# State space mixer: outputs in two kinds of PSUM bank, state tiles made once, second half's transposes in two kinds

## The chip, the core and the metric

The kernel runs on one core of one Trainium2 chip. The metric is device time in microseconds (us) of one launch, the median of several. The core has a matrix engine (TensorE, here PE), three other compute engines (VectorE or DVE, ScalarE or ACT, GpSimd or POOL), and SyncE (SP), whose queue issues the DMAs. PE writes its results to PSUM, eight banks of 128 partitions x 512 float32; DVE and ACT read them out.

## The reference

A transformer block with two mixers, a state space one (S5) and sparse attention, and two feed-forward parts. The change lies in S5. It has 32 groups of 16 channels with 64 complex states each, over 512 time steps:

```python
bu_re = jnp.einsum('bsgc,gpc->bsgp', ug, bbar_re)      # ug: input, 32 groups of 16 channels
bu_im = jnp.einsum('bsgc,gpc->bsgp', ug, bbar_im)
_, _, xr, xi = lax.associative_scan(combine, (a_seq_re, a_seq_im, bu_re, bu_im), axis=1)
y = (jnp.einsum('bsgp,gcp->bsgc', xr, c_re) - jnp.einsum('bsgp,gcp->bsgc', xi, c_im) + d_skip * ug)
yg = jax.nn.gelu(y)
out = yg * jax.nn.sigmoid(yg @ w_glu + b_glu)
```

Beside it stand the gates that later mix the two mixers' outputs: a sigmoid of the normed input times 2048 columns of `w_in`.

## The kernel before

**Gates.** They are computed in 16 units of 128 columns, `gt0_0` to `gt0_7` and `gt1_0` to `gt1_7`. A unit is 24 matmuls of 128x512 that all add into one PSUM bank: eight slices of the inner dimension, each with high part times high part (L211), low times high (L212) and high times low (L213). Weights come by DMA (`raw`); ACT rounds them to the high part `wh`, DVE takes the rest as `wl`. When the 24 are done, DVE scales the bank into `gt` (one 128x512 operation, L192 `gt<-ps_mm,rbs`), which frees the bank, and ACT applies the sigmoid.

**State space.** `s5_half` (L638) handles 16 of the 32 groups at a time, in two tiles `jt` of 8. It is called with `hf` 0 and 1, and the code has it stand between the gates: gates 0 and 1, half 0, gates 2 to 7, half 1, gates 8 to 15, then `glu`. In a half:
- `products` forms the input matrix `T1` (s5A, s5B) and the output matrix `CA` (s5CAr, s5CAi), with a PSUM bank for one factor.
- T1 is transposed on PE (L688) and copied to `W1` by ACT; the products L698 and L699 and the transposes L702 make the kernel `KT` for the four time steps within a chunk. POOL adds the skip term to KT (L734, L735), and ten small DMAs on SP's queue spread it to `G` (L741).
- DVE forms the powers `s5P`.
- For each jt: matmuls L749 of W1 with the input give two banks `wr` and `wi`; DVE turns them by the powers (`turn`, four 128x512 operations), adds and subtracts (two more), runs 8 scans of 128x128 (L773) back into the banks, turns them again (four), and writes the states to `X` (s5Xr, s5Xi, two). Column 0 of X is zero, and POOL sets it (L777).
- The output `py` is 96 small matmuls in one bank (L787): G with the input, CAr with s5Xr, CAi with s5Xi, for four time steps. ACT takes the gelu (`yg`, L790).

**Banks.** The eight banks are dealt by kind (L413): four "mm", one "sm", three "aux". A tile takes the next bank of its kind in the order in which the code asks, and its first writer waits until the bank's former tile has been read for the last time. Gate units are "mm". In a half all of T1, bc, the transposes and KT's products are "aux", wr and wi are "aux" for an even jt and "mm" for an odd one, and py of either jt is "sm".

**What sets the order.** A scheduler orders each engine's instructions from the code, the data they need and the banks; the code adds a few orderings without waits (the `turn` and `before` names). Within one kind of bank, tiles keep the order of the code. An engine works its instructions in order: one that waits holds all behind it.

Of the kernel before, what the change touches and what calls it, by code (L numbers as in the profile page):

```python
# [179 lines left out]
class Kern:  # L180
# [459 lines left out]
    def s5_half(self, hp, hf, A, Gp, m4, u4, s5d, ura):  # L640
        nc, I = self.nc, self.I
# [4 lines left out]
        def tile(shape, name, bufs=1):  # L646
            return hp.tile(shape, F32, name=name, tag=name, bufs=bufs)
# [35 lines left out]
        W1 = [tile([128, 8, 128], n) for n in ("s5W1r", "s5W1i")]  # L683
        for c in range(2):
            for q in range(2):
                tp = self.mmtile((128, 512), "aux")
                for i in range(4):
                    ins = nc.tensor.transpose(tp[:, 128 * i:128 * i + 128], T1[c][:, 4 * q + i], self.ident)  # L688
                    self.tc.add_manual_dep(ins.ins, self.before, NOSYNC, reason="order")
                self.act(W1[c][:, 4 * q:4 * q + 4], tp)  # L690
# [20 lines left out]
        n = 1  # L711
        while n < 128:

            m = min(n, 127 - n)
            if m > 0:
                by = lambda c: PP[:, c:c + 1, :, n:n + 1].to_broadcast([128, 2, 8, m])
                x, o = PP[:, :, :, 1:m + 1], PP[:, :, :, n + 1:n + m + 1]
# [20 lines left out]
        for d in range(4):  # L738
            j = 3 - d
            for s1 in range(4 - d):  # L740
                nc.sync.dma_start(G[32 * s1:32 * s1 + 32, :, s1 + d, :], KT[32 * j:32 * j + 32])  # L741

        for jt in (2 * hf, 2 * hf + 1):
            ur = ura[:, jt]
            q4 = slice(4 * (jt % 2), 4 * (jt % 2) + 4)
            wr, wi = (self.mmtile((128, 512), ("aux", "mm")[jt % 2]) for _ in range(2))
            for c, w in ((0, wr), (1, wi)):
                for pl in range(4):
                    nc.tensor.matmul(w[:, 128 * pl:128 * pl + 128], W1[c][:, q4.start + pl], ur[:, pl],  # L749
                                     start=True, stop=True)  # L750
            Pr, Pi = P[0][:, q4].rearrange("p a b -> p (a b)"), P[1][:, q4].rearrange("p a b -> p (a b)")

            t2 = lambda n: tile([128, 2, 512], n)
            ac = t2("s5A") if jt % 2 == 0 else t2("s5W1r")
            zc = t2("s5C") if jt % 2 == 0 else t2("s5W1i")
            ta, tc = ac[:, 0], ac[:, 1]
            zr, zi = zc[:, 0], zc[:, 1]

            def turn():

                self.tt(ta, wr, Pr, mul)
                self.tt(wr, wr, Pi, mul)
                self.tt(tc, wi, Pr, mul)
                self.tt(wi, wi, Pi, mul)

            turn()
            self.tt(zr, ta, wi, add)
            self.tt(zi, tc, wr, sub)
            for z, s in ((zr, wr), (zi, wi)):
                for pl in range(4):  # L770
                    pr = 4 * jt + pl
                    sl = slice(128 * pl, 128 * pl + 128)
                    nc.vector.tensor_tensor_scan(s[:, sl], m4[:, pr:pr + 1].to_broadcast([128, 128]), z[:, sl], 0.0,  # L773
                                                 mul, add)
            X = [tile([128, 4, 129], n, 1) for n in ("s5Xr", "s5Xi")]
            for x in X:
                nc.gpsimd.memset(x[:, :, 0:1], 0.0)  # L777
            v = lambda a: a.rearrange("p (a b) -> p a b", a=4)
            turn()
            self.tt(X[0][:, :, 1:], v(ta), v(wi), sub)  # L780
            self.tt(X[1][:, :, 1:], v(tc), v(wr), add)

            py = self.mmtile((128, 512), "sm")
            for st in range(4):
                for i, (w, x) in enumerate(((G, ur), (CA[0], X[0]), (CA[1], X[1]))):
                    for pl in range(4):
                        nc.tensor.matmul(py[32 * pl:32 * pl + 32, 128 * st:128 * st + 128], w[:, q4.start + pl, st],  # L787
                                         x[:, pl, 0:128], start=i == 0, stop=i == 2, tile_position=(0, 32 * pl))
            yg = self.gp.tile([128, T], F32, name="yg", tag="yg", bufs=2)
            self.act(yg.rearrange("p (c s) -> p s c", s=4), py.rearrange("p (s c) -> p s c", s=4), AF.Gelu_apprx_tanh)  # L790
            self.split_to(self.y_ssm[0][:, jt], self.y_ssm[1][:, jt], yg)
# [251 lines left out]
    def nsa_cmp(self, p):  # L1043
# [3 lines left out]

        X = p.tile([128, 4, 8, 32], F32, name="cX")
        for half in range(2):
            ps = self.mmtile((128, 512), "aux")  # L1050
            for i2 in range(2):
                i = 2 * half + i2
                for j in range(4):
                    nc.tensor.matmul(ps[:, 256 * i2 + 64 * j:256 * i2 + 64 * j + 64],
                                     qk[j][:, 128 * i:128 * i + 128], self.kcbd, start=True, stop=True)
            self.tt(X[:, 2 * half:2 * half + 2], ps.rearrange("p (a h c) -> p a h c", a=2, h=8),
                    self.biasc[:, 2 * half:2 * half + 2], OP.add)
# [1064 lines left out]
```

## Time and profile before

| | us |
|---|---|
| three runs | 1603.66, 1607.11, 1603.70 |
| median | 1603.7 |
| profiled execution | 1606.45 |
| its span on the engines | 1604.7 |
| PE busy in the span | 1551.7 (97%) |
| DVE busy | 1107.8 (69%) |
| half 0, half 1 and gates 2 to 15, up to the start of `glu` | 54 to 161.28 |

The profiled execution's time is 1.75 above its span and 2.75 above the median of the runs. PE is busy over most of the length; the state space mixer and its gates lie between about 46 and 170 us of the span, and the other 1430 us hold the rest of the block. A matmul's row shows some 0.4 us though the next starts 0.23 later: PE works them in a pipeline, so their cost is read from start to start.

### The profile page before, as it was taken

To read this page: it belongs to the slowest core of one execution; us is meant where nothing else is said; L and a number is where in the kernel's file an instruction comes from. 1 tells how busy PE (TensorE), PEld (TensorE's weight loads), DVE (VectorE), ACT (ScalarE), POOL (GpSimd) and SP (SyncE) were. 2 spreads that over 40 slices of the span, in tenths; PEclk is the share of its full clock that TensorE was granted. 3 is DMA by queue.
4 is the path that set the end of the run, shared out by engine and by line. 5 is a ranking of instruction groups with operands and counts; after the bars stand their busy time and mean duration, and the time that the engine had idled before them with its cause. 6 is when DMAs were issued, how large, how long until landed. Compare 5 with 4: busy or idle time off the path is not lost.

```text
span 1604.7 us, 22771 instructions
## 1 busy us (share of the span) xinstructions
PE 1551.7 (97%) x8577; PEld 1296.0 (81%) x8577; DVE 1107.8 (69%) x2055; ACT 764.3 (48%) x1405; POOL 385.0 (24%) x327
## 2 busy tenths in 40 slices
PE   7999997999999999999999999999989999999997
PEld 6778786677888888888888888878879888888886
DVE  8887546676679754863436777478877798676745
ACT  5453536563444213452346777646654664343322
POOL 1110124113000000000020001314320897556552
PEclk9999999999999999999999999999999999999998
DMA  5222411004356764833222111111211322232322
GB/s 192 82 74 67 133 56 47 14 21 133 103 199 214 245 197 130 258 111 103 82 65 71 33 51 54 47 56 64 66 59 66 102 95 92 98 100 92 96 86 82
DMA packets 58733, 157.84 MB, mean 98 GB/s; under 512 B 11904, under 2 KB 18816, under 8 KB 58496
## 3 DMA queue, kind: packets, MB, share of 16 engines
q1 hardware_dynamic: 58624, 156.40, 30.4%
q8 instruction: 67, 1.10, 0.3%
q14 instruction: 42, 0.34, 0.1%
HBM read 152.57 MB, written 2.10 MB: 96 GB/s over the span
## 4 chain that ended last, share of the span: by engine, by line
PE 81%; DVE 11%; ACT 5%; issue 2%; POOL 1%; DMA 1%; SPq 0%; DVEq 0%; ACTq 0%
PE ps_mm L211 23%; PE ps_mm L213 22%; PE ps_mm L212 22%; PE ps_sm L1129 2%; DVE wl L192 2%; DVE caccm L201 2%; PE ps_mm L1118 1%; PE ps_aux L1574 1%; ACT L189 1%; ACT wh L189 1%; PE ps_sm L787 1%; DVE caccf L201 1%; PE ps_aux L1563 1%; PE ps_aux L1096 1%; PE ps_sm L1590 0%
## 5 line engine op out<-in xcount | busy, mean ns | idle before, releaser
L189 ACT ACTIVATE wh<-raw 128x1024 fp32r<-128x1024 f32 (+3 forms) x234 | 236.8, 1013 | 498.7 <-PE ps_mm L212 361.6
L192 DVE TENSOR_TENSOR wl<-raw,wh 128x1024 fp32r<-128x1024 f32 (+2 forms) x162 | 196.7, 1215 | 99.3 <-ACT wh L189 93.5
L201 DVE SCALAR_TENSOR_TENSOR caccf<-ps_mm,cwf,caccf 128x441 f32<-128x441 f32 (+2 forms) x278 | 188.5, 695 | 30.9 <-ACT ctapf L189 24.8
L192 POOL TENSOR_TENSOR wl<-raw,wh 128x1024 fp32r<-128x1024 f32 (+2 forms) x72 | 160.7, 2233 | 158.7 <-ACT wh L189 158.6
L213 PE MATMUL ps_mm<-h4H,wl 128*128 128x512 f32 (+1 forms) x352 | 131.2, 375 | 0.0
L212 PE MATMUL ps_mm<-h4L,wh 128*128 128x512 f32 (+1 forms) x352 | 131.1, 375 | 0.0
L211 PE MATMUL ps_mm<-h4H,wh 128*128 128x512 f32 (+1 forms) x352 | 129.7, 377 | 0.6 <-DVE caccf L201 0.4
L192 POOL TENSOR_TENSOR rr<-rv,nhalf 128x2 f32<-128x2 f32 x9 | 8.5, 946 | 431.3 <-DVE rv L198 431.3
L211 PE MATMUL ps_mm<-h2H,wh 128*128 128x512 f32 (+1 forms) x280 | 103.8, 372 | 0.0
L213 PE MATMUL ps_mm<-h2H,wl 128*128 128x512 f32 (+1 forms) x280 | 103.6, 371 | 0.0
L212 PE MATMUL ps_mm<-h2L,wh 128*128 128x512 f32 (+1 forms) x280 | 103.6, 371 | 0.0
L211 PE MATMUL ps_mm<-aH,wh 128*128 128x512 f32 (+1 forms) x272 | 102.6, 377 | 0.5 <-DVE x L192 0.5
L213 PE MATMUL ps_mm<-aH,wl 128*128 128x512 f32 (+1 forms) x272 | 102.7, 378 | 0.0
L212 PE MATMUL ps_mm<-aL,wh 128*128 128x512 f32 (+1 forms) x272 | 102.4, 377 | 0.0
L1265 DVE CUSTOM_DVE_ANT_0 msc<-wmod,cB,cols 128x1024 bf16<-128x1024 f32 x64 | 82.0, 1282 | 21.1 <-DMA wmod<-in_wmod 20.7
L211 PE MATMUL ps_mm<-hH,wh 128*128 128x512 f32 x216 | 85.2, 402 | 8.2 <-ACT hH L189 8.2
L213 PE MATMUL ps_mm<-hH,wl 128*128 128x512 f32 x216 | 85.4, 396 | 1.5 <-DVE wl L192 1.5
L212 PE MATMUL ps_mm<-hL,wh 128*128 128x512 f32 x216 | 85.4, 396 | 0.0
L213 PEld LDWEIGHTS ps_mm<-h4H,wl 128*128 128x128 f32 x352 | 66.2, 188 | 12.3
L212 PEld LDWEIGHTS ps_mm<-h4L,wh 128*128 128x128 f32 x352 | 66.2, 188 | 12.3 <-DVE h4L L201 0.4
L211 PEld LDWEIGHTS ps_mm<-h4H,wh 128*128 128x128 f32 x352 | 65.0, 188 | 13.4 <-issue 0.8
L211 PE MATMUL ps_mm<-faH,wh 128*128 128x512 f32 (+1 forms) x194 | 72.3, 373 | 0.0
(548 smaller groups left out, 4039.2 us busy)
## 6 DMA issues: line engine op xcount, KB each, us to landing
raw<-in_wup SPq DMA_DIRECT2D x76, 512.0 KB, 3.5
wmod<-in_wmod SPq DMA_DIRECT2D x48, 512.0 KB, 4.3
raw<-in_wdn SPq DMA_DIRECT2D x32, 512.0 KB, 3.5
raw<-in_win SPq DMA_DIRECT2D x28, 512.0 KB, 3.3
raw<-in_wout SPq DMA_DIRECT2D x8, 512.0 KB, 3.5
raw<-in_wdn2a SPq DMA_DIRECT2D x8, 512.0 KB, 3.5
raw<-in_wdn2b SPq DMA_DIRECT2D x8, 512.0 KB, 3.4
raw<-in_wdn2c SPq DMA_DIRECT2D x8, 384.0 KB, 3.2
```

Source lines behind the costliest of these rows:

```text
L189: return self.nc.scalar.activation(o, i, f, **k)
L192: return (e or self.nc.vector).tensor_tensor(o, a, b, op)
L201: return self.nc.vector.scalar_tensor_tensor(o, a, s, b, op0, op1)
L211: mm(ps, wh, xh, start=start, stop=False)
L212: mm(ps, wh, xl, start=False, stop=False)
L213: ins = mm(ps, wl, xh, start=False, stop=stop)
L787: nc.tensor.matmul(py[32 * pl:32 * pl + 32, 128 * st:128 * st + 128], w[:, q4.start + pl, st], x[:, pl, 0:128], start=i == 0, stop=i == 2, ...
L1096: nc.tensor.matmul(S[:, :n2], self.qs[:, 2 * j + g, c], self.ks[:, 2 * br + g, :n2], start=True, stop=False)
L1118: nc.tensor.transpose(tp[:, 128 * b:128 * b + 128], P[g, i][:, 128 * b:128 * b + 128], self.ident)
L1129: nc.tensor.matmul(O[64 * g:64 * g + 64, 128 * i:128 * i + 128], self.V[:, b, c:c + 64], PT[g][:, 128 * b:128 * b + 128], start=br == 0 an ...
L1265: ins = nc.vector.tensor_tensor_reduce(sc, w, cB[:, c], 1.0, bm[:, m:m + 1], OP.mult, OP.add, acc)
L1563: nc.tensor.matmul(ps[k0:k0 + m, j, c:c + m], e[:, k0:k0 + m], e[:, q0:q0 + m], start=True, stop=True, tile_position=(0, k0), skip_group_c ...
```

## The change

1. In the second half two of the four transposed tiles of T1 (q = 1) go to "mm" banks and not to "aux".
2. The state tiles X are made once, in the first half, and their zero column is set once. Before, every jt made them and set the column.
3. py of an odd jt goes to an "mm" bank; only the even jt's goes to "sm".

```diff
@@ s5_half: transposes of T1
         for c in range(2):
             for q in range(2):
-                tp = self.mmtile((128, 512), "aux")
+                tp = self.mmtile((128, 512), ("aux", "mm")[hf and q])
@@ s5_half: before the loop over jt
+        if hf == 0:
+
+            self.s5X = [tile([128, 4, 129], n, 1) for n in ("s5Xr", "s5Xi")]
+            for x in self.s5X:
+                nc.gpsimd.memset(x[:, :, 0:1], 0.0)
         for jt in (2 * hf, 2 * hf + 1):
...
-            X = [tile([128, 4, 129], n, 1) for n in ("s5Xr", "s5Xi")]
-            for x in X:
-                nc.gpsimd.memset(x[:, :, 0:1], 0.0)
+            X = self.s5X
...
-            py = self.mmtile((128, 512), "sm")
+            py = self.mmtile((128, 512), ("sm", "mm")[jt % 2])
```

Lines below the insertion have other numbers afterwards: L749 becomes L754, L773 becomes L778, L787 becomes L790.

The change also moves instructions. The numbers behind names tell tiles apart. First PE in the first half, before: `ps_aux_668` and `669` are wr and wi of jt 0, `ps_mm_757` and `758` those of jt 1, `ps_sm_704` is py of jt 0, `ps_mm_852` and `885` are the banks of gates 2 and 3.

```order
L211 MATMUL ps_mm_852<-hH_78,wh_848 128x512
...
L702 MATMUL ps_aux_567<-ident_76,s5ks_576 128x128 [waits Activation_49]
L212 MATMUL ps_mm_852<-hL_79,wh_848 128x512
...
L702 MATMUL ps_aux_580<-ident_76,s5ks_589 128x128 [waits Activation_49]
...
L213 MATMUL ps_mm_852<-hH_78,wl_849 128x512
L211 MATMUL ps_mm_885<-hH_78,wh_881 128x512 [waits DVE_49]
...
L749 MATMUL ps_aux_668<-ur_123,s5W1r_540 128x128 [waits DVE_49,PE_49,Activation_49]
...
L749 MATMUL ps_aux_669<-ur_123,s5W1i_541 128x128 [waits DVE_49]
...
L787 MATMUL ps_sm_704<-ur_123,s5G_656 32x128 [waits DMAHW3_49,Pool_49]
```

The same place of the changed kernel: `ps_aux_672` and `673` are wr and wi of jt 0, `ps_mm_789` is py of jt 1, `ps_mm_848`, `881` and `914` are the banks of gates 2, 3 and 4.

```order
L702 MATMUL ps_aux_567<-ident_76,s5ks_576 128x128 [waits Activation_49]
L702 MATMUL ps_aux_580<-ident_76,s5ks_589 128x128 [waits Activation_49]
L754 MATMUL ps_aux_672<-ur_123,s5W1r_540 128x128 [waits DVE_49,PE_49,Activation_49]
...
L754 MATMUL ps_aux_673<-ur_123,s5W1i_541 128x128 [waits DVE_49]
...
L790 MATMUL ps_sm_704<-ur_123,s5G_656 32x128 [waits DMAHW3_49,Pool_49]
...
L790 MATMUL ps_mm_789<-ur_123,s5G_656 32x128 x4
L211 MATMUL ps_mm_848<-hH_78,wh_844 128x512
...
L211 MATMUL ps_mm_881<-hH_78,wh_877 128x512 [waits DVE_49]
...
L211 MATMUL ps_mm_914<-hH_78,wh_910 128x512 [waits DVE_49]
```

The 44 matmuls of gates 2 and 3 that stood among and behind L702, ahead of L749, now stand behind the first matmuls of both py. In before four "mm" tiles are live here (wr, wi and two gate banks in turn); now py of jt 1 holds a third bank for as long, the gates have one bank left, and gates 3, 4 and 5 each start with a wait for DVE's read of the gate ahead. The second half has the same form: the first matmul of gate 8 follows the first four of py of jt 3, and gates 9, 10 and 11 each wait for DVE's read of the gate ahead.

DVE at the same place, before:

```order
L192 TENSOR_TENSOR ps_aux_645<-s5Ap_367,ps_aux_518 128x512 [waits Activation_49]
L192 TENSOR_TENSOR gt0_2_402<-ps_mm_852,rbs_124 128x512 [waits PE_49]
L201 SCALAR_TENSOR_TENSOR ps_aux_645<-s5t_644,ps_aux_645 128x512 [waits DVE_49]
...
L192 TENSOR_TENSOR s5A_678<-ps_aux_669,s5P_593 128x512 [waits PE_49]
L192 TENSOR_TENSOR ps_aux_669<-ps_aux_669,s5P_593 128x512
L192 TENSOR_TENSOR gt0_3_403<-ps_mm_885,rbs_124 128x512 [waits PE_49]
...
L773 SCALAR_TENSOR_TENSOR ps_mm_757<-s5s_301,s5W1i_768 128x128 [waits DVE_49]
L773 SCALAR_TENSOR_TENSOR ps_mm_758<-s5s_301,s5W1i_768 128x128
L192 TENSOR_TENSOR wl_948<-raw_945,wh_947 128x1024 [waits DMAHW5_49,Activation_49]
L192 TENSOR_TENSOR gt0_4_404<-ps_mm_918,rbs_124 128x512 [waits PE_49]
```

And of the changed kernel:

```order
L778 SCALAR_TENSOR_TENSOR ps_mm_758<-s5s_301,s5W1i_768 128x128
L192 TENSOR_TENSOR gt0_2_402<-ps_mm_848,rbs_124 128x512 [waits PE_49]
L778 SCALAR_TENSOR_TENSOR ps_aux_672<-s5s_301,s5C_683 128x128 [waits DVE_49]
...
L192 TENSOR_TENSOR wl_944<-raw_941,wh_943 128x1024 [waits DMAHW5_49,Activation_49]
...
L778 SCALAR_TENSOR_TENSOR ps_aux_673<-s5s_301,s5C_683 128x128 [waits DVE_49]
L192 TENSOR_TENSOR s5W1r_767<-ps_mm_757,s5P_593 128x512 [waits DVE_49]
...
L192 TENSOR_TENSOR ps_aux_673<-ps_aux_673,s5P_593 128x512
L192 TENSOR_TENSOR gt0_3_403<-ps_mm_881,rbs_124 128x512 [waits PE_49]
L192 TENSOR_TENSOR wl_977<-raw_974,wh_976 128x1024 [waits DMAHW6_49,Activation_49]
```

The read of gate 2 now follows the first two of the 16 scans, and that of gate 3 the other 14 scans, one `wl`, one `s5nci` (L197) and the eight operations of the second turns, where gates 2, 3 and 4 were read among the operations ahead of the third scan. In the second half gate 8 is read after four scans, and gate 9 after the other twelve, a `wl` and the second turns. `gt0_4` comes after the X tiles, 7 large and some small operations of half 1.

## Rows read from the trace of the kernel before

**Rows 1.** The page: span, busy time and share of each engine
```profile
span 1604.7 us, 22771 instructions
PE 1551.7 (97%) x8577; PEld 1296.0 (81%) x8577; DVE 1107.8 (69%) x2055; ACT 764.3 (48%) x1405; POOL 385.0 (24%) x327
```

**Rows 2.** Waits of PE, 40 to 190 us: total us, times, longest us
```profile
PE ps_sm L787 <- ACT yg L189: 1.7, 1, 1.7
PE ps_aux L688 <- ACT s5W1r L189: 1.7, 2, 1.0
PE ps_mm L213 <- DVE wl L192: 1.5, 1, 1.5
...
PE ps_aux L688 <- POOL s5Xi L777: 0.9, 1, 0.9
PE ps_sm L787 <- DVE s5Xr L192: 0.6, 1, 0.6
```

**Rows 3.** Timeline of PE, pieces of 54 to 162: start us, us, instruction
```profile
55.38 0.27 PE L702 MATMUL ps_aux<-ident,s5ks 128*128 128x128 f32 x1
...
55.95 0.39 PE L211 MATMUL ps_mm<-hH,wh 128*128 128x512 f32 x1
56.18 0.39 PE L212 MATMUL ps_mm<-hL,wh 128*128 128x512 f32 x1
...
65.40 1.05 PE L749 MATMUL ps_aux<-ur,s5W1r 128*128 128x128 f32 x8
...
103.48 0.66 PE L688 MATMUL ps_aux<-ident,s5A 128*128 128x128 f32 x4
...
108.69 0.48 PE L211 MATMUL ps_mm<-hH,wh 128*128 128x512 f32 x1
...
161.28 0.40 PE L211 MATMUL ps_mm<-ysH,wh 128*128 128x512 f32 x1
```

**Rows 4.** Timeline of DVE, pieces of 61 to 76
```profile
61.44 0.68 DVE L192 TENSOR_TENSOR ps_aux<-s5Ap,ps_aux 128x512 f32<-128x512 f32 x1
62.03 0.68 DVE L192 TENSOR_TENSOR gt<-ps_mm,rbs 128x512 f32<-128x512 f32 x1
...
74.34 0.74 DVE L773 TENSOR_TENSOR_SCAN ps_mm<-s5s,s5W1i 128x128 f32<-128x128 f32 x2
74.99 1.21 DVE L192 TENSOR_TENSOR wl<-raw,wh 128x1024 fp32r<-128x1024 f32 x1
```

**Rows 5.** Timelines of ACT, POOL and SP's queue, 59 to 68
```profile
59.77 1.20 ACT L189 ACTIVATE s5CAr<-ps_aux 64x512 f32<-64x512 f32 x2 [1.40 <-DVE ps_aux L192]
...
58.51 0.94 POOL L192 TENSOR_TENSOR s5KT<-s5KT,s5ks 32x128 f32<-32x128 f32 x1 [0.44 <-ACT s5KT L189]
...
61.11 6.47 SPq L741 DMA_DIRECT2D s5G<-s5KT  x10
```

**Rows 6.** DMA issues, 50 to 70: count, KB each, us from issue to landing
```profile
s5G<-s5KT SPq DMA_DIRECT2D x10, 32.0 KB, 1.9
```

**Rows 7.** Timeline of PE, outputs of jt 0 and jt 1, 93 to 102
```profile
93.66 0.40 PE L787 MATMUL ps_sm<-ur,s5G 128*32 128x128 f32 x8
93.88 0.40 PE L787 MATMUL ps_sm<-s5Xr,s5CAr 128*32 128x128 f32 x8
...
99.06 0.43 PE L787 MATMUL ps_sm<-ur,s5G 128*32 128x128 f32 x8 [1.73 <-ACT yg L189]
...
101.05 0.68 PE L787 MATMUL ps_sm<-ur,s5G 128*32 128x128 f32 x8
101.48 0.68 PE L787 MATMUL ps_sm<-s5Xr,s5CAr 128*32 128x128 f32 x8
```

**Rows 8.** Busy time by stretch: PE, PEld, DVE, ACT, POOL, then PE's granted clock
```profile
76.00:92.00 16.00, 15.74 (x69) 12.85 (x70) 16.00 (x32) 4.97 (x6) 0.15 (x2) 1.00 0.34 110
...
97.00:104.00 7.00, 5.27 (x105) 4.84 (x103) 6.83 (x23) 4.56 (x7) 0.93 (x2) 0.76 0.23 75
...
280.00:288.00 8.00, 6.99 (x33) 4.74 (x34) 5.66 (x16) 1.71 (x5) 1.74 (x1) 0.57 0.00 0
```

## The prediction

> **What bounds the kernel.** I read the page first: PE is busy for 1551.7 of 1604.7 us [rows 1], so a change pays by taking idle time from PE and costs by adding it. Next comes the list of PE's waits around the changed code [rows 2]: 1.7 for `yg` and 0.6 for s5Xr ahead of the outputs, 1.7 in two pieces for W1 and 0.9 for POOL ahead of the transposes, 1.5 for a `wl`. Of the two pieces for W1 the larger (1.0) comes before 54 us, outside the stretch; the other 0.7 and all the rest lie in it. So 1.7 + 0.6 + 0.7 + 0.9 + 1.5 = 5.4 us is all that can be had there by waiting less. The timeline of PE shows what fills the time beside the state space work: gate matmuls, 0.23 us from start to start, 24 to a gate, 5.5 us [rows 3]. And the timeline of DVE shows that turns and scans come one behind the other with no gap [rows 4].
>
> **The edits that cost little.** Six of eight zero columns are no longer set. The waits show 0.9 for POOL's s5Xi ahead of a transpose [rows 2], and I count that as gained at most. Transposes in two kinds of bank can gain the 0.7 for W1. Both are in the 5.4.
>
> **py in an "mm" bank.** In before py of jt 1 waits until the gelu has read py of jt 0: 1.73 us at 99.06. Behind that stop the groups of eight output matmuls start 0.43 apart (101.05 to 101.48) where those of jt 0 start 0.22 apart [rows 7], and the granted clock of 97 to 104 is 0.76 [rows 8]: 7 x 0.24 = 1.7 us more. With its own bank py of jt 1 waits for nothing, and both losses can go.
>
> The Trainium skill (Perfetto Trace Analysis, "Optimizing Tensor Performance", Matmuls) says that independent groups of matmuls should rotate through different PSUM banks, so that reading one overlaps the next group. For py the trace agrees (1.73 us in one bank). By that rule applied to py alone the change gains; but the same rule speaks against it for the gates, which lose a bank.
>
> **What the gates lose.** The changed order decides this. wr and wi of jt 1 and its py hold three of the four "mm" banks from before gate 2 until the gelu, and the gates have one. Two things follow. The first gate's matmuls stand behind the first matmul of py, which waits for G; and gate n+1 waits until DVE has read gate n, which on DVE stands among the turns and scans. I walk this with durations from before: 5.5 a gate, 12 groups x 0.22 = 2.6 an output block, 0.60 a 128x512 on DVE (61.44 to 62.03), 0.65 two scans, 1.13 a `wl` (1.21 less the 0.08 by which neighbours overlap) [rows 3, 4, 7].
>
> 1. *Ahead of gate 2.* PE is through with L702 at about 55.6; in before gate matmuls fill the time to L749 at 65.40 [rows 3]. Now wr waits for the copy of CAr, which ends at 59.77 + 1.20 = 60.97; wi for the read of bc at 61.44, done at 62.0; py for the first copies into G, 61.11 + 1.9 = 63.0 [rows 4 to 6]. With the matmuls themselves (8 of 128x128 twice, 1.05 by the row [rows 3], some 0.9 apart; two groups of outputs, 0.4) gate 2 starts at about 64.1. Of these 8.5 us PE works 2.3: idle 6.2.
> 2. *Gate 3.* Gate 2 runs 64.1 to 69.6. The read of a gate at 62.03 goes, the last product takes its place, and DVE is through with the products at 62.6. Then come 13 operations of 0.60 (7.8) and two scans (0.65): 71.1, and the read ends at 71.7. Idle 2.1.
> 3. *Gate 4.* Gate 3 ends at 77.2. DVE has from 71.7 on 14 scans (4.55), a `wl` (1.13), s5nci (0.2, estimated from its size), eight operations (4.8) and the read (0.6): 11.3, to 83.0. Idle 5.8.
> 4. *Gate 5.* Gate 4 to 88.5, then the output of jt 0 to 91.0. DVE's read of gate 4 comes after a `wl` (1.1), eight large operations (4.8), some thirteen small ones (0.2 each, 2.6, an estimate) and itself (0.6): 9.1 after 83.0, 92.1 at most. I take 0.5: the output block is the cover, and without it this is 3 more.
> 5. *Ahead of gate 8.* Gates 5 to 7 and the output of jt 1 follow without a wait, to about 110.6. Transposes, KT's products and wr, wi of jt 3 take 5 us: from 103.48 to 108.69 is 5.2 [rows 3], less 0.7 of waiting, plus one transpose of 0.5. Then the same chain as in step 1 (copy, two products, CAr 1.2; POOL's adds of 0.94, four copies into G at 0.65, landing 1.9 [rows 5, 6]). G is the later, some 6.5 us after L702, of which PE works 2.5. Idle 4.0.
> 6. *Gate 9.* DVE gets through 12 operations and four scans (8.5) while gate 8 runs (5.5, from three to four us later): idle 0.7.
> 7. *Gate 10.* 12 scans (3.9), a `wl`, eight operations and the read: 10.4 against 5.5 of gate 9. Idle 4.9.
>
> From gate 11 on DVE is ahead again, and `glu` and the rest stand in the order of before. New idle: 6.2 + 2.1 + 5.8 + 0.5 + 4.0 + 0.7 + 4.9 = 24.2.
>
> **The clock.** Behind the stop of 1.73 PE ran a while at the lower of its two levels and lost 1.7 [rows 7, 8]; in 280 to 288, behind another stop, the granted clock is 0.57, a loss of 8 x 0.43 = 3.4 [rows 8]; behind the 1.5 for `wl` [rows 2], just before 76.3, the clock of 76 to 92 is 1.00 [rows 8]. So a stop of 4 to 6 us should cost 0 to 3.4, and I take 1.7, the row nearest to it in kind. After steps 1 and 5 DVE's wait that follows hides it (2.1 and 0.7); after steps 3 and 7 nothing does: 0 + 1.7 + 0 to 1 + 1.7, some 3.5, between 0 and 8.
>
> The Trainium skill (TensorE: Matmul & The Clock Gate, "What's actually happening") says that the throttled state is the default and that activity releases it. By that page a loss behind steps 3 and 7 is to be expected; the trace agrees for outputs (0.76), and no row of before shows it for a gate behind so long a stop. Without it the sum would be 3.5 lower.
>
> **Sum.** 24.2 new idle - 5.4 old idle - 1.7 old loss of clock + 3.5 new loss = +20.6. The walk in time gives a little less: gate 10 starts at about 139, then 6 gates and two outputs make 177 without losses of clock, against 161.28 [rows 3]; +15.7, with 3.5 for the clock +19.2. I take +19.5. On the profiled execution (1606.45, span 1604.7 and 1.75 around it) that makes 1626; the median of the runs stands 2.75 lower, so I forecast 1603.7 + 19.5 = **1623.2**.
>
> **Rivals.**
> - *The clock stays up, and DVE comes to its reads sooner.* +24.2 - 7.1 = +17.1 without any loss of clock; should the small operations of step 4 and the chain of step 5 be 3 us shorter, +14: 1618 to 1620. For it: the clock of 76 to 92. Against: rows 8.
> - *The clock falls for longer.* 3.4 for each of the four long stops, not hidden where DVE isn't the later: +26 to +30, 1630 to 1634. For it: 280 to 288. Against: in 97 to 104 the same thing cost half of that, and 0.57 is the lowest clock among these stretches.
> - *Made good later.* Everything after `glu` waits for PE, and 97% of the span is PE's [rows 1]. If a later wait of PE is for DMA, or for work that DVE does beforehand, it shrinks by up to what is late. 53 us of idle time stand in the whole span, so the 19 could be lost among it; but weights are loaded ahead and DVE's reads follow PE's results, so I expect little. To come within 4.8 us (0.3%, what a measurement of this kernel can tell from no change) 15 must be made good: 1600 to 1608.
> - *Faster.* One mechanism: the single "sm" bank with its stop at 99.06. If the new waits of gates are hidden, the 5.4 and the 1.7 remain, -7.1: 1596.6. It decides if gate 2 starts by 57 instead of 64 and the reads of gates come as soon as a gate ends. For it: PE's waits of before all lie at py and the transposes [rows 2]. Against: in the changed order no gate matmul stands between L702 and py's first, and 16 scans don't vanish.
> - *It doesn't do what it says.* Should py of jt 3 still wait for the gelu, 2 to 3 us stay: 1625, inside the range.
>
> **Chances.** The forecast with a spread of 1619 to 1628: 0.56. Clock up or DVE sooner, 1612 to 1619: 0.18. Clock down for longer, 1628 to 1635: 0.13. Made good later: 0.08. Faster: 0.05. The range of 1611 to 1632 leaves out the last two and the top of the third, about 0.18. Slower by over 0.3%: 0.56 + 0.18 + 0.13 = 0.87; within: 0.08; faster: 0.05.
>
> **What would show it.** On PE: an idle time of 4 to 5 us each ahead of the first L754 on "aux" in both halves, and a shorter one ahead of the first L790 or wi; gate matmuls (L211) with idle time released by DVE `gt`, two long ones (near 6 and 5 us) and short ones; none for `yg` any more. On the clock: granted values under 0.9 in stretches behind 83 and 139. `glu` starts near 180 instead of 161.28, and from there on every row stands later by the same amount. The forecast is wrong if PE has no such idle time (the order on the chip then lets gates through), if the two long waits are under 3 us each (DVE faster through its turns than rows of before say), or if `glu` is 19 late and the end is not.

## The result and the profile after

The changed kernel takes 1627.19 us, median of four runs (1625.75 to 1628.58), against 1603.95 for the kernel before beside it: a ratio of 1.0139, 95% interval 1.0123 to 1.0156, slower by 22 us. The profiled execution took 1625.91, its span 1624.2 (1604.7 before [rows 1]).

The page's first lines: span, then busy time and share of each engine.

```profile
span 1624.2 us, 22752 instructions
PE 1554.1 (96%) x8577; PEld 1296.6 (80%) x8577; DVE 1109.0 (68%) x2055; ACT 763.7 (47%) x1405; POOL 383.5 (24%) x321
```

PE has the same 8577 matmuls. The span grew by 19.5 us and PE's busy time by 2.4 alone, so most of the loss is idle time. The list of PE's waits from 40 to 210 us says where (what PE wanted to do, whom it waited for, total us, times, longest):

```profile
PE ps_mm L211 <- DVE gt L192: 11.6, 4, 5.4
PE ps_aux L754 <- ACT s5CAr L189: 5.3, 1, 5.3
PE ps_aux L754 <- DVE ps_aux L192: 3.0, 1, 3.0
PE ps_aux L688 <- ACT s5W1r L189: 1.6, 2, 1.0
PE ps_aux L688 <- issue: 1.4, 2, 0.9
```

Three lines are new, 11.6 + 5.3 + 3.0 = 19.9 us. Of the old ones [rows 2] those for yg, s5Xr, POOL and `wl` are gone. So is the one for W1 in the second half (0.7): the waits for W1 and the two put down to `issue` that are left all stand ahead of 54 us. PE's timeline shows the starts of the pieces that matter (start us, us of the row, instruction, idle time before it and its releaser):

```profile
59.85 2.07 PE L754 MATMUL ps_aux<-ur,s5W1r 128*128 128x128 f32 x8 [5.25 <-ACT s5CAr L189]
...
64.57 0.52 PE L211 MATMUL ps_mm<-hH,wh 128*128 128x512 f32 x1
...
71.18 0.50 PE L211 MATMUL ps_mm<-hH,wh 128*128 128x512 f32 x1 [0.88 <-DVE gt L192]
...
76.53 0.39 PE L213 MATMUL ps_mm<-hH,wl 128*128 128x512 f32 x1
82.33 0.80 PE L211 MATMUL ps_mm<-hH,wh 128*128 128x512 f32 x1 [5.41 <-DVE gt L192]
82.92 0.63 PE L212 MATMUL ps_mm<-hL,wh 128*128 128x512 f32 x1
83.35 0.63 PE L213 MATMUL ps_mm<-hH,wl 128*128 128x512 f32 x1
...
88.74 0.39 PE L211 MATMUL ps_mm<-hH,wh 128*128 128x512 f32 x1
88.97 0.40 PE L212 MATMUL ps_mm<-hL,wh 128*128 128x512 f32 x1
...
121.66 1.18 PE L754 MATMUL ps_aux<-ur,s5W1r 128*128 128x128 f32 x8 [3.01 <-DVE ps_aux L192]
...
125.50 0.76 PE L211 MATMUL ps_mm<-hH,wh 128*128 128x512 f32 x1
...
132.29 0.50 PE L211 MATMUL ps_mm<-hH,wh 128*128 128x512 f32 x1 [0.78 <-DVE gt L192]
...
142.60 0.50 PE L211 MATMUL ps_mm<-hH,wh 128*128 128x512 f32 x1 [4.53 <-DVE gt L192]
...
182.50 0.39 PE L211 MATMUL ps_mm<-ysH,wh 128*128 128x512 f32 x1
```

Gate 2 starts at 64.57, gate 3 at 71.18, gate 4 at 82.33; in the second half gates 8, 9 and 10 at 125.50, 132.29 and 142.60. Behind 82.33 the gate matmuls start 0.43 apart (82.92 to 83.35), and only from 88.7 on 0.23. `glu` starts at 182.50, 21.2 later than in before [rows 3]. DVE's timeline shows what gate 4 waited for:

```profile
70.46 0.67 DVE L192 TENSOR_TENSOR gt<-ps_mm,rbs 128x512 f32<-128x512 f32 x1
...
76.83 0.67 DVE L192 TENSOR_TENSOR s5W1r<-ps_mm,s5P 128x512 f32<-128x512 f32 x1
...
81.00 0.68 DVE L192 TENSOR_TENSOR ps_aux<-ps_aux,s5P 128x512 f32<-128x512 f32 x1
81.60 0.68 DVE L192 TENSOR_TENSOR gt<-ps_mm,rbs 128x512 f32<-128x512 f32 x1
...
91.02 0.69 DVE L192 TENSOR_TENSOR gt<-ps_mm,rbs 128x512 f32<-128x512 f32 x1 [1.39 <-PE ps_mm L213]
```

Gate 2 is read at 70.46, gate 3 at 81.60, behind 14 scans, one `wl` and the eight operations of the second turns, with no gap between. The last of gate 3's matmuls had started at 76.53, so its result lay ready for some 5 us before DVE came to it. At 91.02 it is DVE that waits, for gate 4.

The stretches behind the four long stops follow (from and to in us, length, then busy us of PE, PEld, DVE, ACT and POOL); the value behind POOL's is the granted clock:

```profile
59.80:64.60 4.80, 4.75 (x33) 4.11 (x33) 4.42 (x8) 1.78 (x3) 0.00 (x0) 0.50 0.23 43
82.00:91.00 9.00, 8.67 (x28) 6.66 (x32) 7.60 (x23) 3.22 (x6) 0.99 (x1) 0.64 0.17 58
121.60:126.00 4.40, 4.34 (x33) 3.70 (x34) 3.80 (x8) 1.19 (x3) 0.00 (x0) 0.62 0.32 54
142.00:150.00 8.00, 7.40 (x32) 5.71 (x35) 4.12 (x7) 0.86 (x2) 0.00 (x0) 0.79 0.18 66
```

By length times what is missing to 1.00 the lower clock cost 2.4 + 3.2 + 1.7 + 1.7 = 9.0 us. The balance up to `glu` is then 19.9 of new idle time - 5.4 of old - 1.7 of old clock + 9.0 of new = +21.8, against 21.2 measured. Behind `glu` 1.7 come back in this pair of executions. Most of it (1.5) stands in one stretch of 40 us, first before and then after, where the granted clock was 0.96 the one time and 1.00 the other:

```profile
761.28:801.28 40.00, 37.63 (x206) 32.41 (x205) 18.75 (x37) 13.01 (x23) 1.44 (x2) 0.96 0.28 91
```

```profile
782.50:822.50 40.00, 37.61 (x213) 32.48 (x212) 19.84 (x39) 13.85 (x25) 1.44 (x2) 1.00 0.28 89
```

### The profile page after: what moved, and what is told of

Same layout as the page of the kernel before. It is cut to its first block, busy times and chain, and to the rows that moved or that the text cites. A ratio compares the mean times of both kernels' runs of the same rounds, so it can differ in the third digit from the quotient of the medians.

```text
span 1624.2 us, 22752 instructions
## 1 busy us (share of the span) xinstructions
PE 1554.1 (96%) x8577; PEld 1296.6 (80%) x8577; DVE 1109.0 (68%) x2055; ACT 763.7 (47%) x1405; POOL 383.5 (24%) x321
## 4 chain that ended last, share of the span: by engine, by line
PE 81%; DVE 11%; ACT 4%; issue 2%; POOL 1%; DMA 1%; SPq 0%; DVEq 0%; ACTq 0%; POOLq 0%
PE ps_mm L211 23%; PE ps_mm L213 22%; PE ps_mm L212 22%; PE ps_sm L1132 2%; DVE caccm L201 2%; DVE wl L192 2%; PE ps_mm L1121 1%; PE ps_aux L1577 1%; ACT wh L189 1%; ACT L189 1%; DVE caccf L201 1%; PE ps_aux L1566 1%; DVE ps_aux L192 1%; PE ps_aux L1099 1%; PE ps_sm L1593 0%
## 5 line engine op out<-in xcount | busy, mean ns | idle before, releaser
L211 PE MATMUL ps_mm<-hH,wh 128*128 128x512 f32 x216 | 87.6, 413 | 19.8 <-DVE gt L192 11.6
```

The source lines that it names most:

```text
L211: mm(ps, wh, xh, start=start, stop=False)
```

## Experiments

All ratios are against the kernel before beside them on the same chip, with 95% intervals.

### py alone, and all but py

The first version, py alone, puts only the last line of the change into the kernel before.

```diff
-            py = self.mmtile((128, 512), "sm")
+            py = self.mmtile((128, 512), ("sm", "mm")[jt % 2])
```

Expected: 

> The kernel before with one part of the change alone: py of an odd jt in an mm bank. Theory (py holds the bank that the gates need): the whole loss, +20 to +24 us, about 1626, with the same two long waits of gates for DVE's read (5.4 and 4.5 us). Rival (the transposes in mm banks or the X tiles made once carry a part): clearly less than +20.

Measured: 1.0115 (1.0099 to 1.013), 1625.13 against 1606.16: +18.5 by the ratio, a little under the expected span. Its waits from 40 to 220 us are those of the changed kernel:

```profile
PE ps_mm L211 <- DVE gt L192: 11.4, 4, 5.4
PE ps_aux L749 <- ACT s5CAr L189: 5.3, 1, 5.3
PE ps_aux L749 <- DVE ps_aux L192: 3.0, 1, 3.0
```

In the second half the gates' two waits have changed places: 4.35 ahead of gate 9 and 0.90 ahead of gate 10. `glu` starts at 181.65, 20.4 later than in before. py is the loss.

The second version, all but py, is the changed kernel with that line undone. Expected: 

> The changed kernel with py back in the sm bank: transposes in two kinds and X made once are left. Theory: between -2 and +1 us against before, 1602 to 1605, since the waits for POOL (0.9) and W1 (0.7) are all that these parts can give, and the outputs' waits are of another kind. Rival (the two mm banks of the transposes delay the gates of half 1): +3 or more, with waits of gates for ACT.

Measured: 0.9979 (0.997 to 0.9989), 1603.33 against 1606.16. It ran again later, beside other versions. Expected: 

> The version without py in mm once more, beside the next one on the same chip. Expected 0.997 to 0.999 of before as at first.

Measured: 0.9984 (0.9975 to 0.9992). These two parts gain some 3 us, which is more than the waits that the first expectation counted (0.9 and 0.7). The gain doesn't show beside py: 18.5 less 3 is not the 22 of the whole change, and no run says how much of that gap is the spread between two comparisons.

Which of the two parts gains? X made once, alone. Expected: 

> The kernel before with one part alone: X made once, its zero column set once. The wait for POOL's s5Xi (0.9) ahead of a transpose was counted as gained. In the versions without py in mm a wait of 0.89 stays at that place and is put down to nothing that the profile shows. Theory now (the column was not what the transpose waited for): 0.999 to 1.001 of before. Rival (first count): 0.9994 or less, that is 0.9 us, too little to be told from the first, so the row of the wait decides: it stays or goes.

The transposes alone (the first line of the change). Expected: 

> The kernel before with one part alone: the second half's transposes in two kinds of bank. Theory: the wait of 0.7 for W1 goes, the transposes follow one another; 0.9985 to 1.000. Together with X made once it should give what the version without py in mm gave (0.998). Rival (the two mm banks delay gate 8): 1.001 or more.

Measured: X once 0.9999 (0.999 to 1.0007), transposes 0.9982 (0.9973 to 0.9991). PE's timeline at the disputed wait, first X once, then transposes alone:

```profile
96.76 0.63 PE L688 MATMUL ps_aux<-ident,s5A 128*128 128x128 f32 x4 [0.89 <-issue]
...
99.11 0.43 PE L790 MATMUL ps_sm<-ur,s5G 128*32 128x128 f32 x8 [1.73 <-ACT yg L189]
103.61 0.66 PE L688 MATMUL ps_aux<-ident,s5B 128*128 128x128 f32 x4 [0.65 <-ACT s5W1r L189]
```

```profile
97.79 0.63 PE L688 MATMUL ps_aux<-ident,s5A 128*128 128x128 f32 x4 [0.89 <-POOL s5Xi L777]
100.15 0.42 PE L787 MATMUL ps_sm<-ur,s5G 128*32 128x128 f32 x8 [1.29 <-ACT yg L189]
```

Without POOL's column the 0.89 stays and loses only its releaser's name: the transpose never waited for the column. The transposes in two kinds end the wait for W1 (0.65) and shorten the one for yg by 0.44. By the ratios they are the whole gain of the two parts. These two rows make 1.1 of the some 3 us; where the rest comes from is not shown.

### The late start by itself

Here the changed kernel has py back in "sm". An extra tile takes the "mm" bank where py of an odd jt asked, gets four small matmuls of G, and is read early (ACT reads it at 65.6 and 119.4). So gates 2 and 8 start late, but the gates behind them have two banks.

```diff
+            if jt % 2:
+                hold = self.mmtile((128, 512), "mm")
+                for pl in range(4):
+                    nc.tensor.matmul(hold[32 * pl:32 * pl + 32, 0:128], G[:, q4.start + pl, 0], ur[:, pl, 0:128],
+                                     start=True, stop=True, tile_position=(0, 32 * pl))
...
+            if jt % 2:
+                self.act(tile([128, 8], "s5hold"), hold[:, 0:8])
```

Expected: 

> The changed kernel with py in sm, and where py of the odd jt asked for an mm bank an extra tile asks for one: four small matmuls of G go there and ACT reads a piece early, so it is given back soon; the extra work is not part of the reference. Gate 2 and gate 8 stand behind these matmuls as in the changed kernel, but the gates behind them have two banks. Theory (late start of the gates costs by itself): waits of 5.3 and 3.0 us ahead of wr, a low clock behind them, some 8 to 13 us above before, no wait of a gate for DVE over 2 us. Rival (the late start is hidden because DVE sets the pace, and the gates' waits are the whole loss): 0 to 4 above before.

Measured: 1.0045 (1.0031 to 1.0059), +7.2 us by the ratio, just under the expected 8 to 13; `glu` starts at 169.60, 8.3 later than in before. Its waits:

```profile
PE ps_aux L754 <- ACT s5CAr L189: 5.3, 1, 5.3
PE ps_aux L754 <- DVE ps_aux L192: 3.0, 1, 3.0
...
PE ps_aux L698 <- ACT s5W1i L189: 1.5, 1, 1.5
PE ps_mm L211 <- DVE gt L192: 1.5, 2, 0.8
```

The first two are those of the changed kernel to the tenth, and the waits for a gate's read are 1.5 where they were 11.6. This version keeps the transposes in two kinds, so what it adds is read against the version without py in mm (0.9979 and 0.9984, `glu` at 159.56 and 158.58): the late start of gates 2 and 8 costs some 10 us, the 1.5 for W1i among them, which that version doesn't have. From here to the changed kernel it is 12.9 us at `glu` (169.60 to 182.50) and some 15 by the ratios. That part comes with the single bank behind the late start. The rival (the gates' waits are the whole loss) falls.

### Each half by itself

```diff
-            py = self.mmtile((128, 512), ("sm", "mm")[jt % 2])
+            py = self.mmtile((128, 512), ("sm", "mm")[jt == 3])
```

Expected: 

> The changed kernel, but py goes to an mm bank in the second half alone (jt 3). Theory: each half loses by itself, and the second lost 3.0 + 0.8 + 4.5 us of waiting and some 3 us of clock: +10 to +12, about 1615; the first half has gates in two banks as in before and its stop for yg of 1.7. Rival (the first half's late start of gate 2 carries it all and the second only follows): +3 or less.

Measured: 1.012 (1.0103 to 1.0138), +19: the second half alone loses nearly what both lose together, and both expectations miss. PE's timeline, and below it one row of DVE's:

```profile
111.92 0.66 PE L790 MATMUL ps_sm<-ur,s5G 128*32 128x128 f32 x8 [5.84 <-DMA s5G<-s5KT]
...
119.96 1.05 PE L754 MATMUL ps_aux<-ur,s5W1r 128*128 128x128 f32 x8
...
126.65 0.50 PE L211 MATMUL ps_mm<-hH,wh 128*128 128x512 f32 x1 [4.04 <-DVE gt L192]
...
140.60 0.80 PE L211 MATMUL ps_mm<-hH,wh 128*128 128x512 f32 x1 [6.58 <-DVE gt L192]
```

```profile
121.12 0.69 DVE L192 TENSOR_TENSOR s5A<-ps_aux,s5P 128x512 f32<-128x512 f32 x1 [7.87 <-PE ps_aux L754]
```

The stops are 16.5 us together, where the changed kernel has 8.3 in its second half. The rows show that PE's order differs. Here the first outputs (111.92) and gate 8 (from 112.93) stand ahead of wr and wi of jt 2 (119.96); in the changed kernel wr comes first (121.66), then the outputs (124.48) and gate 8 (125.50). So here PE has nothing to do while the outputs wait for G, and DVE stands idle for 7.87 us until wr is there. Its turns start late, and gate 8's read and gate 9 behind it wait for them.

DVE was also later with the powers of this half: its last operation on s5P started at 110.05, 7 us behind the first wr of that half at 103.01; in the changed kernel it started at 101.15, 14 us ahead of that wr at 115.60, since PE was late there already. No run separates this lead from the order. What is shown is that the losses of two places don't add: a part of a change, measured alone, is not its share of the whole.

### Who asks first

Here gate units are written ahead of py of the odd jt, so that they ask for their banks before it does, five in either half (the lines of the second half read alike):

```diff
-        self.s5_half(hp, 0, *par, s5d, ur)
-        self.gates(hs, 0, (2, 8))
+        self.s5_half(hp, 0, *par, s5d, ur, lambda: self.gates(hs, 0, (2, 7)))
+        self.gates(hs, 0, (7, 8))
...
+            if jt % 2:
+                mid()
             py = self.mmtile((128, 512), ("sm", "mm")[jt % 2])
```

Expected: 

> The changed kernel, but five gate units are written ahead of py of the odd jt in either half, so that they ask for their mm banks before py does; the computation is the same. Theory (who asks first has the bank): gates rotate over two banks during turns and scans again, no wait of a gate for DVE's read over 2 us, no stop for yg; 1598 to 1602, 2 to 6 below before. Rival (a bank fewer hurts whoever asks first): the loss moves to py and the time stays above 1612.

Measured: 1.0012 (1.0002 to 1.0021). The loss of 22 shrinks to 2, but the expected gain doesn't come. The largest wait left is that of gate 7, the one unit of the half left behind py:

```profile
90.82 0.77 PE L211 MATMUL ps_mm<-hH,wh 128*128 128x512 f32 x1 [3.65 <-DVE gt L192]
```

Behind it the granted clock was 0.50 (90 to 95), 2.5 us more. With six ahead (all of gates 2 to 7, and gates 8 to 13), expected: 

> The changed kernel with six gate units written ahead of py of the odd jt in either half, so that no gate of the first half asks for a bank after py. The five-gate version still had one wait of 3.65 us there, of gate 7, and a lower clock behind it. Theory: that wait goes, the stop for yg (1.3 without py in mm) stays away too; against before a ratio of 0.995 to 0.998, 1 to 4 us below the version without py in mm (0.998). Rival (py then waits for a gate's read, and the stop only changes its name): 0.998 to 1.001, with 1 us or more of waiting ahead of the odd py.

Measured: 0.9986 (0.9977 to 0.9995), in the rival's span. Gate 7's wait is gone, and the odd py waits for its own X, not for a gate's read as the rival had it:

```profile
98.45 0.43 PE L791 MATMUL ps_mm<-s5Xr,s5CAr 128*32 128x128 f32 x8 [0.70 <-DVE s5Xr L192]
99.27 0.43 PE L791 MATMUL ps_mm<-s5Xi,s5CAi 128*32 128x128 f32 x8 [0.39 <-DVE s5Xi L192]
```

Once more beside the version without py in mm, expected: 

> The version with six gate units ahead of py, once more, to be compared on one chip with the version without py in mm. By the start of glu (158.8 against 159.6) it should be 0.8 us faster, 0.9965 to 0.9985; if its time is above the other's, the extra bank for py gains nothing that lasts.

Measured: 0.9985 (0.9977 to 0.9994), 1603.07, against 1602.30 for that version; `glu` starts at 160.44 here and at 158.58 there, so the 0.8 us is gone too. A bank of its own for py shows no gain, even where no gate of the first half has to wait for it.

### Other banks

One version puts py of the odd jt in "aux". Expected: 

> The changed kernel with py of the odd jt in an aux bank. Theory (what counts is which work loses the bank): gates keep two mm banks, no gate waits over 2 us for DVE, no stop for yg; the second half's products have an aux bank less, and they have time: ratio 0.995 to 0.999. Rival (any bank that py holds through the turns stalls someone on PE's path): 1.004 or more, with PE waiting for the transposes or wr of the second half.

Measured: 0.9995 (0.9985 to 1.0005), no difference from before, and between the two expectations. No gate waits for a read, and the stop for yg is gone, but this stands in its place:

```profile
99.23 0.43 PE L790 MATMUL ps_aux<-s5Xr,s5CAr 128*32 128x128 f32 x8 [2.04 <-DVE s5Xr L192]
```

Another has five "mm" banks and two "aux", with py as changed (`self.PB = {"mm": 5, "sm": 1, "aux": 2}`). Expected: 

> The changed kernel with five mm banks and two aux banks; py of the odd jt in mm. Theory (the gates lack one bank, no more): gates rotate again, no wait for DVE's read over 2 us between 55 and 165, glu starts between 155 and 166 instead of 182.5. What two aux banks cost in the rest of the block is not known, so the time says little. Rival (the loss is py's place in the order, not the number of banks): glu starts after 175.

Measured: 1.0416 (1.0402 to 1.043), +67 us, of which 15.4 stand ahead of `glu`. Of its waits from 40 to 220:

```profile
PE ps_aux L688 <- DVE wl L192: 4.2, 1, 4.2
PE ps_aux L754 <- DVE ps_aux L192: 3.8, 1, 3.8
PE ps_sm L790 <- DMA s5G<-s5KT: 3.8, 1, 3.8
PE ps_aux L698 <- ACT s5W1i L189: 2.6, 2, 1.9
```

No gate waits for DVE's read any more, as the theory had it; but `glu` starts at 176.67, outside its span, and the waits are now at the products and transposes, which have a bank less. The rival named the start of `glu`, and met it, for another reason than it gave. Neither of these two deals of the eight banks serves gates, outputs and products alike.

## Why the prediction was right

The prediction forecast +19.5 (1623.2, within 1611 to 1632); measured were +22 by the ratio and a median of 1627.19. The mechanism was the one that the runs show: py takes the gates' second bank, so gates start late and then wait for reads that stand among turns and scans. Step by step, with the forecast first:

- *Ahead of gate 2*: 6.2 of idle time and a start at 64.1 forecast, 5.25 and 64.57 measured. L754 and the first outputs ran at half the rate (granted clock 0.50), which took back what the stop was shorter, and the second, shorter stop ahead of wi or the outputs didn't come.
- *Gate 3*: 2.1 forecast, 0.88 measured, since gate 2 ended 0.5 later and DVE got to its read at 70.46 and not at 71.1.
- *Gate 4*: 5.8 and 5.41. DVE's chain of scans, `wl`, turns and read, 11.3 by rows of before, took 11.1 (70.46 to 81.60).
- *Gate 5*: 0.5 and none: at the lower clock gate 4 took 8.6 us (82.33 to 90.9), and DVE's work up to that read, 9.1 forecast, took 8.0 (81.60 to 89.6), so DVE was ready first.
- *Ahead of gate 8, gates 9 and 10*: 4.0, 0.7 and 4.9; measured 3.01, 0.78 and 4.53.
- *Sum of new idle time*: 24.2 against 19.9, 4.3 too much.
- *The clock*: the term that was mis-sized, 3.5 against 9.0. I charged 1.7 each behind gates 4 and 10 (3.2 and 1.7 measured) and held the losses behind steps 1 and 5 (2.4 and 1.7) to be hidden by the waits that follow. In small part they were: the wait of step 2 came out 1.2 shorter, 0.5 of it since gate 2 came later, and that of step 6 no shorter. The two errors, 4.3 too much idle time and 5.5 too little for the clock, nearly cancel; that the sum came so near is in part luck.
- *Old losses that go*: the 5.4 of idle time and the 1.7 went in this kernel, where PE was late anyway; a bank of its own for py doesn't by itself give them. Where py has a bank of its own and the gates keep theirs, the stop for yg turns into one for s5Xr (2.04 with "aux", 0.70 + 0.39 with six gates ahead). "A stall goes, say what is late next" was the question here, and the forecast didn't ask it for py. Nor did POOL's column cost the 0.9 that its row names.

Of the rivals, *the clock falls for longer* was right on the size behind gate 4 (3.2, with 3.4 given), but its 26 to 30 took the idle time at its forecast size. *Made good later* and *faster* fell: of the 21.2 at `glu` 19.5 are there at the end. That the whole of -7.1 could be had with the gates' waits hidden is refuted by the two versions with gates ahead: 0.9986 and 0.9985.

The Trainium skill's rule on rotating banks (Perfetto Trace Analysis, "Optimizing Tensor Performance", Matmuls) holds here for the gates: one bank in place of two cost 11.6 us of waiting for reads. For py, which the rule seemed to favour, no run shows a gain.

The lowest ratios belong to versions that leave py in "sm": transposes in two kinds alone (0.9982), or with X made once (0.9979 and 0.9984). Those with six gates ahead (0.9986 and 0.9985) can't be told from them.

## What to carry to other kernels

A PSUM bank given to one tile is taken from another: before moving a tile to another kind of bank, list which tiles of that kind are live while it is, from its first write to its last read, and in which order they ask. A group whose reader is busy with a long chain needs two banks, or reads that stand ahead of that chain (which no run here tried by itself). And price a stall that goes by what is late behind it, not by its length: here 1.7 us of waiting for a bank hid 1 to 2 us of waiting for the data.

## What the hardware showed that was not expected

The loss of clock behind a short stop comes and goes with the same program. The version without py in mm was profiled twice, on two chips. It has a stop of 1.28 us for yg the first time and of 1.29 the second. The stretch around and behind it is, the first and the second time:

```profile
97.00:104.00 7.00, 5.72 (x108) 5.28 (x107) 6.70 (x23) 5.04 (x8) 0.97 (x2) 0.76 0.26 80
```

```profile
97.00:104.00 7.00, 5.47 (x129) 4.70 (x129) 6.86 (x23) 6.69 (x11) 1.92 (x3) 1.00 0.23 77
```

The clock was 0.76 once and 1.00 once, 1.7 us apart; X once, with a stop of 1.73 as long as that of before [rows 7], ran on at the full rate. So the 1.7 of the sum did not follow from the length of that stop.

Longer stops are no surer. In the changed kernel's profile the clock fell behind each stop of 3.0 to 5.4 us, and the loss didn't follow their length (3.2 behind 5.41, 1.7 behind 4.53, 2.4 behind 5.25). The stop of 3.0 ahead of wr in the second half stands in three programs: behind it the granted clock was 0.62 in the changed kernel (121.6 to 126) and 0.58 in the version with the extra tile (115 to 119), but 1.00 with py alone (122 to 127). Part of the spread of runs, 3 to 7 us within one kernel, may come from this; no run separates it.
